# A hybrid encoder layer in float32: seven column blocks instead of four in the first stage of the feed-forward block, biases first, x by column blocks

## The chip, the cores and the metric

The kernel runs on one core of one Trainium2 chip. The metric is device time in microseconds (us) of one execution, as the median of several; lower is better. All arithmetic is float32: each large product is done on TensorE in three passes over operands that are split into a high and a low part.

## The reference

One encoder layer over 256 tokens of 2048 features (`SEQ` 256, `D_MODEL` 2048, `D_FF` 8192, one layer, so only the attention mixer occurs):

```python
mod = silu(c) @ mod_w + mod_b                       # 2048 -> 6 x 2048
sh_m, sc_m, g_m, sh_f, sc_f, g_f = split(mod, 6)
h = x * (1 + sc_m) + sh_m
x = layer_norm(ALPHA * x + (1 + g_m) * attention(h))  # q 32 heads, k and v 8 heads of 64, |q-k| <= 128, sink
h = x * (1 + sc_f) + sh_f
u = square(relu(h @ w1 + b1))                       # 2048 -> 8192
x = layer_norm(ALPHA * x + (1 + g_f) * (u @ w2 + b2)) # 8192 -> 2048
```

The weights are some 280 MB, read once: `mod_w` in 96 loads of 1 MB, the QKV matrix in 24, the output projection in 16, `w1` and `w2` in 64 each.

## The kernel before

**Weights.** Every weight comes as a 128x2048 float32 tile `raw` of 1 MB, issued in one fixed order on SP's queue (L580). Eight such buffers exist early, five later. For a matrix product each half of a tile is split: ScalarE copies it to the rounded high part `wh` (L638 while the order is written out, L627 later), VectorE subtracts to get the low part `wl` (L596). Five halves of each fit. A product of x and w is three matmuls, high by high, high by low, low by high (`mm3`, L925 to L927, 512 columns).

**Modulations.** A load of `mod_w` is used in one of two ways. As a *column*, VectorE multiplies it with the broadcast activation `cb` and sums along the row (`Col.step`, L742): one instruction for each load, which holds the scale, the shift or the gate of 128 features. As a *product*, TensorE does it (`Mod.quad`, L703, groups of 32 matmuls), with a small row turned afterwards. `MIXP` says which of the 16 attention feature tiles use the product, `FFP` how many per feature group of the feed-forward (before: two in group 2, so four product loads).

**Order written out by a planner.** `FLOW` is a hand-written list of loads: `"m"` two attention modulation loads, a number or `(g, p)` a QKV chunk, `"g"` and `"G"` the attention gate as column or product, `("o", c, j)` a chunk of the output projection, `"f"` and `"p"` a feed-forward modulation as column or product, `"x"` the rows of x for the residual, `"F"` a chunk of `w1`. `flow_order` takes that list with a table of costs (`COST`) and returns the order of every instruction on every engine up to the first `w1` chunks; the kernel issues them in exactly that order (`P` pins it). Where PE has nothing to do at the start and in the LayerNorm chain, dummy matmuls are issued (`idle`, L1041 and L1043).

**Biases.** The biases of QKV and of the output projection are added by a matmul with a selecting stationary operand (`bq`, L532), before as the last step of each sum.

**Attention, output projection, LayerNorm.** Scores (L1096), masking and maximum (L1105), exponential (L1113), scaling (L1136), transposes (L1142), values (L1161). The output projection is accumulated by 512-column block `c`; `gated_sum` forms gate times result (L1375), adds ALPHA x (L1377) and takes statistics (L1379). Then `norm_part`, `normed` (L1219, L1222), `ff_turn` transposes (L1280) and `ff_input` scales, splits (L1294, L1296, L1292) into the 16 input tiles of the feed-forward, by four feature groups.

**Feed-forward, first matrix.** The first 2048 hidden features (`w1a`) are done by *feature group*: chunk `W1A[n] = (kg, fq)` multiplies input group `kg` (512 features) with column block `fq` (512 hidden features) in the three-pass form with 256 columns (`w1a_unit`, L1316 to L1318), so that group 0 can start before groups 1 to 3 are there. Partial sums leave PSUM by L1329 (first) or L1326 (added), unless `KEEP` holds them there. The other hidden features are done tile by tile (`ff_hidden`): per input tile one 512-column matmul of `wh` with the high and low input side by side (L1539) and one 256-column matmul of `wl` (L1541), alternating eight and eight.

**Feed-forward, second matrix.** In four rounds (`BLK`) of 2048 hidden features, four chunks for each 512-column block `c` of the output (`ff_out`, again `mm3`). Between rounds the sums are added to `ys` (L1579, L1581). The last round is gated and normed while it ends.

Of the kernel before, what the change touches and what calls it, by code (L numbers as in the profile page):

```python
# [46 lines left out]
def mod_chunks():  # L47
# [8 lines left out]
    for which, p in (("m", GMP), ("f", 0)):  # L56
# [18 lines left out]
COST = dict(gP=1.01, gD=2.212, r=.2, c=.2, a=.1, H=.51, T=.33, S=.34, h=.96, l=1.137, u=1.36, e=.6, E=.48, sp=.85,  # L75
            cp=.48, bq=.5, rm=1.25, ra=1.2, ht=.43, hc=.48, sc=1.07, tt=.405, es=.2, ee=.1, ex=.49, rs=.19, rc=.09,
# [4 lines left out]
MODE = dict(u=0, w=0, bq=0, gP=2, sc=2, va=2)  # L81
TURN = (0.0, .11, .2, -.07, 0.0, .1, .15, .15, 0.0)
LATER = dict(gD=.3, gP=.1, u=.1, w=.1)
BANKS = dict(sum=6, gv=1, q=1, lt=2, wo=4, pm=1, sc=2, pt=2, po=1, w1=6)
W1A = [(0, 0), (0, 1), (0, 2), (0, 3), (1, 0), (1, 1), (1, 2), (1, 3),
       (2, 0), (2, 1), (2, 2), (2, 3), (3, 0), (3, 1), (3, 2), (3, 3)]
KEEP = ((0, 0), (0, 1), (2, 0), (2, 1))


def flow_loads():  # L90
# [3 lines left out]
    cols = [("gc", k) for k in range(4 * GMP, NK)]  # L94
    ff = [[v for v in ff_chunks() if v[2] == p] for p in range(2)]
    for v in FLOW:
# [5 lines left out]
        elif v == "g":  # L102
            out.append(cols.pop(0))
        elif v in ("f", "p"):
            out.append(("f",) + ff[v == "p"].pop(0))
        elif v == "x":
            out.append(("x",))
# [14 lines left out]
def flow_order():  # L122
# [28 lines left out]
    done, halves, freed, last, opened, out_of, summed = {}, [], [], {}, {}, {}, {}  # L151
    zs = [n for n in weights if type(n) is tuple and n[0] == "o"][-2:]
    for n in weights:
# [3 lines left out]
        for x in range(2):  # L157
            h, l = ("h", n, x), ("l", n, x)
            op(h, "ACT", "h", [("w", n)] + [("h",) + v for v in halves[-1:]], 1)
            op(l, "DVE", "l", [h] + [("l",) + v for v in halves[-1:]], 1, (), (), x == 1)  # L160
# [10 lines left out]
        for n, i in units:  # L171
            after = [("l", n, i % 2 if kind in "qz" else i // 2)] + last.get(kind == "u", [])
# [5 lines left out]
            elif kind == "w":  # L178
                kg, fq = W1A[n[1]]
                after += [("fc", kg, kp, x) for kp in range(2) for x in range(2)]  # L180
# [3 lines left out]
            if kind == "u" and k == 0:  # L184
                banks = ("sum",) * 2
            elif kind == "q" and i % 2 == 0:
                banks = ("q",)
            elif kind == "l" and i == 0 and n[1] not in opened:
                banks, opened[n[1]] = ("lt",) * 2, 1
            elif kind2 == "o" and i == 0 and n[1] not in out_of:  # L190
                banks, out_of[n[1]] = ("wo",) * 2, 0
            elif kind == "w" and (kg - 1, fq) not in KEEP and i % 2 == 0:
                banks = ("w1",)
            op(("u", n, i), "PE", "w" if kind == "w" else "u", after, 3, banks)
            if kind == "w" and (kg, fq) not in KEEP and i % 2:
                if fq in summed:
                    op(("ev", kg, fq, i // 2), "DVE", "ed", [("u", n, i), ("ev", summed[fq], fq, i // 2)], 1, (), ("w1",))
                else:
                    op(("ev", kg, fq, i // 2), "ACT", "ev", [("u", n, i)], 1, (), ("w1",))
# [9 lines left out]
            if kind == "u" and k == NK - 1 or kind == "l" and n[0] == 3 and i == 3:  # L209
                p = p if kind == "u" else n[1]  # L210
                op(("bq", p), "PE", "bq", [("u", n, i), ("sv",)], 1)
# [1553 lines left out]
```

## Time and profile before

| | |
|---|---|
| median of 3 runs | 1065.18 us (1064.52 to 1066.4) |
| profiled execution | 1064.04 us, span 1062.3 us |
| PE busy | 1041.4 us (98%) |
| DVE busy | 817.2 us (77%) |
| ACT busy | 535.9 us (50%) |
| POOL busy | 17.4 us (2%) |
| read from HBM | 288.5 MB |

PE is TensorE's matmul queue, DVE VectorE, ACT ScalarE, POOL GpSimd, SP the queue that issues the weight loads. A line such as `L742` is the kernel's line. Times in the views are microseconds from the start of the span, then the duration. "x8" means that so many instructions are merged in the row, and brackets at the end say how long the engine had been idle and what it waited for. Matmuls are pipelined and their ends modelled, so the distance of their starts, not their duration, is their price; a PE that is busy by the table may still have small gaps.

### The profile page before, as it was taken

The numbers are of one execution on the slowest core, as the hardware profiler recorded it, in microseconds if no ns is written. First come the engines' busy times: TensorE is split into PE (matmuls) and PEld (weight loads), VectorE is DVE, ScalarE is ACT, GpSimd is POOL, SyncE is SP. The second block draws the span as 40 slices with busy tenths as digits, with TensorE's granted clock in tenths as the row PEclk, the third lists the DMA queues.
The fourth block names the chain that finished last, engine by engine and source line by source line (L and its number), as shares of the span: only waits on it lengthen the run. The fifth ranks groups of instructions, "written<-read, shape, count | busy, mean of one in ns | idle before, by whom it ended". The sixth has DMA issues, their size and how long they took to land.

```text
span 1062.3 us, 15134 instructions
## 1 busy us (share of the span) xinstructions
PE 1041.4 (98%) x5955; PEld 872.2 (82%) x5955; DVE 817.2 (77%) x1137; ACT 535.9 (50%) x831; POOL 17.4 (2%) x41
## 2 busy tenths in 40 slices
PE   8899999999998999999999999999999999999997
PEld 6678787767886999888888888888888888888885
DVE  3989999999999999755778788666655566665795
ACT  4354469998335646633455543345443334454340
POOL 1000000000000000000000010000000000000000
PEclk9999999999999999999999999999999999999999
DMA  9999995589999997556877888856555555557512
GB/s 376 418 423 419 422 420 208 219 314 382 420 382 366 401 381 253 185 198 203 309 276 260 296 301 295 310 193 215 194 192 188 185 193 199 193 198 249 191 76 79
DMA packets 43463, 291.63 MB, mean 275 GB/s; under 512 B 4940, under 2 KB 5100, under 8 KB 9600
## 3 DMA queue, kind: packets, MB, share of 16 engines
q1 hardware_dynamic: 40256, 281.82, 70.2%
q0 software_dynamic: 2272, 7.40, 2.2%
q10 hardware_dynamic: 864, 1.45, 0.4%
q8 instruction: 46, 0.75, 0.3%
q14 instruction: 25, 0.20, 0.1%
HBM read 288.54 MB, written 2.11 MB: 274 GB/s over the span
## 4 chain that ended last, share of the span: by engine, by line
PE 70%; DVE 14%; DMA 11%; ACT 4%; issue 1%; DVEq 0%; ACTq 0%
PE pa L1539 17%; PE pa L925 12%; PE pa L927 12%; PE pa L926 12%; PE pa L1541 9%; DMA raw<-in_wqkv 6%; DVE raw L742 5%; DVE wl L596 4%; PE pa L1316 2%; PE pa L1318 2%; PE pa L1317 2%; DMA raw<-in_mod 2%; DMA raw<-in_wo 1%; DVE g L1105 1%; ACT g L1113 1%
## 5 line engine op out<-in xcount | busy, mean ns | idle before, releaser
L596 DVE TENSOR_TENSOR wl<-raw,wh 128x1024 fp32r<-128x1024 f32 x332 | 401.9, 1222 | 185.2 <-ACT wh L627 175.8
L627 ACT CAST wh<-raw 128x1024 fp32r<-128x1024 f32 x226 | 238.0, 1053 | 318.7 <-PE pa L927 184.5
L925 PE MATMUL pa<-wh,g 128*128 128x512 f32 x816 | 322.3, 395 | 2.0 <-ACT g L1021 1.4
L926 PE MATMUL pa<-wl,g 128*128 128x512 f32 x816 | 318.9, 391 | 2.0 <-DVE wl L596 2.0
L927 PE MATMUL pa<-wh,g 128*128 128x512 f32 x816 | 318.7, 391 | 1.0 <-DVE g L960 0.9
L1539 PE MATMUL pa<-g,wh 128*128 128x512 f32 x768 | 192.3, 392 | 0.0
L742 DVE CUSTOM_DVE_ANT_0 raw<-raw,cb 128x2048 f32<-128x2048 f32 x78 | 177.6, 2284 | 13.0 <-DMA raw<-in_mod 12.8
L925 PEld LDWEIGHTS pa<-wh,g 128*128 128x128 f32 x816 | 153.5, 188 | 39.2 <-issue 3.6
L927 PEld LDWEIGHTS pa<-wh,g 128*128 128x128 f32 x816 | 153.6, 188 | 34.3 <-DVE g L960 1.3
L926 PEld LDWEIGHTS pa<-wl,g 128*128 128x128 f32 x816 | 153.7, 188 | 33.6 <-DVE wl L596 2.8
L638 ACT CAST wh<-raw 128x1024 fp32r<-128x1024 f32 x106 | 109.5, 1052 | 100.0 <-PE pa L927 36.3
L1539 PEld LDWEIGHTS pa<-g,wh 128*128 128x128 f32 x768 | 138.3, 189 | 25.0 <-ACT wh L627 0.2
L1541 PEld LDWEIGHTS pa<-g,wl 128*128 128x128 f32 x768 | 104.8, 190 | 7.5
L1541 PE MATMUL pa<-g,wl 128*128 128x256 f32 x768 | 107.1, 282 | 0.0
L1316 PE MATMUL pa<-g,wh 128*128 128x256 f32 x256 | 72.8, 285 | 0.5 <-ACT g L1294 0.5
L1318 PE MATMUL pa<-g,wl 128*128 128x256 f32 x256 | 72.4, 283 | 0.0
L1317 PE MATMUL pa<-g,wh 128*128 128x256 f32 x256 | 72.4, 283 | 0.0
L1316 PEld LDWEIGHTS pa<-g,wh 128*128 128x128 f32 x256 | 49.1, 192 | 0.8 <-ACT g L1294 0.8
L1317 PEld LDWEIGHTS pa<-g,wh 128*128 128x128 f32 x256 | 49.1, 192 | 0.0
L1318 PEld LDWEIGHTS pa<-g,wl 128*128 128x128 f32 x256 | 49.1, 192 | 0.0
L1113 ACT ACTIVATE g<-g,nm 128x256 f32<-128x256 f32 x64 | 32.5, 530 | 1.2 <-DVE nm L1105 1.1
L1136 ACT ACTIVATE g<-g,rs 128x256 f32<-128x256 f32 x64 | 28.4, 532 | 0.0
(198 smaller groups left out, 695.0 us busy)
## 6 DMA issues: line engine op xcount, KB each, us to landing
raw<-in_mod SPq DMA_DIRECT2D x96, 1024.0 KB, 8.8
raw<-in_w SPq DMA_DIRECT2D x64, 1024.0 KB, 4.9
raw<-in_w1b SPq DMA_DIRECT2D x48, 1024.0 KB, 4.8
raw<-in_wqkv SPq DMA_DIRECT2D x24, 1024.0 KB, 16.3
raw<-in_wo SPq DMA_DIRECT2D x16, 1024.0 KB, 9.9
raw<-in_w1a SPq DMA_DIRECT2D x16, 1024.0 KB, 7.7
g<-in_x SPq DMA_DIRECT2D x4, 512.0 KB, 8.1
gb<-in_lnrow POOLq DMA_DIRECT2D x8, 256.0 KB, 5.5
```

Source lines behind the costliest of these rows:

```text
L596: self.pinned(nc.vector.tensor_sub(l, r, f32(self.hs[n])))
L627: self.last[n] = nc.scalar.copy(h, s)
L638: self.pinned(nc.scalar.copy(h, s))
L742: S.pinned(nc.vector.tensor_tensor_reduce(out=raw, in0=raw, in1=cb, scale=1.0, scalar=0.0, op0=OP.mult, op1=OP.add, accum_out=self.dst))
L925: S.pinned(nc.tensor.matmul(ps, xh, wh, start=start, stop=False))
L926: S.pinned(nc.tensor.matmul(ps, xh, wl, start=False, stop=False))
L927: S.prev = nc.tensor.matmul(ps, xl, wh, start=False, stop=stop)
L1316: S.pinned(nc.tensor.matmul(o, wh(w, 128), hh, start=new and fi + k == 0, stop=False))
L1317: S.pinned(nc.tensor.matmul(o, wh(w, 128), hl, start=False, stop=False))
L1318: S.pinned(nc.tensor.matmul(o, wl(w, 128), hh, start=False, stop=end and fi == 1 and k == 3))
L1539: nc.tensor.matmul(ps, wh(k, 128), ff_in(k), start=k == 0, stop=False)
L1541: nc.tensor.matmul(ps[:, :256], wl(k, 128), ff_in(k)[:, :256], start=False, stop=k == NK - 1)
```

## The change

1. `w1a` has seven column blocks (`NW1A` 7) in place of four: 28 chunks by feature group (7 for each group, in orders of their own, with new `KEEP`), and 36 hidden tiles in place of 48 in `ff_hidden`. The rounds of the second matrix take 3, 4, 5 and 4 chunks per column block (`BLOCKS`). The squares of blocks 0 to 2 follow their sums; those of blocks 3 to 6 come in the last column block of round 0. The columns of the second gate move from the second round to the third.
2. The first `w1a` chunk is done in halves of its input group, so that it begins when two of the group's four input tiles are there.
3. `FFP` is zero: all 32 feed-forward modulation loads are columns on VectorE. `MIXP` has tiles 0, 1, 2, 3, 10 in place of 0, 1, 2, 8, 12.
4. `FLOW` is new: the output projection's chunks come earlier in it, the feed-forward modulations later; 22 `w1` chunks are in it in place of 13.
5. The bias matmul opens a sum (`start`) in place of closing it; its loads and split come first.
6. x comes in four loads, one for each `"x"` in `FLOW`, from a layout with the column block outermost; before, one `"x"` issued four.
7. `ys` is loaded with the second bias directly, in eight broadcast loads on POOL's queue; before, two loads and an addition in the first round.
8. The table for the exponential is loaded by a one-element activation right after the sines.
9. `ff_hidden` does the 16 wide matmuls of a tile, then the 16 narrow ones.
10. Some costs of the planner change.

```diff
-BLK = 4
+NW1A = 7
+BLOCKS = ((0, 3), (3, 4), (7, 5), (12, 4))
-MIXP = tuple(int(k in (0, 1, 2, 8, 12)) for k in range(16))
+MIXP = tuple(int(k in (0, 1, 2, 3, 10)) for k in range(16))
-FFP = (0, 0, 2, 0)
+FFP = (0, 0, 0, 0)
 FLOW = [
+    "m", "m", 0, 1, "m", "m", (0, 4), 2, (0, 5), "m", "m", 3, "m", (0, 3), 4, "m", (1, 3), (1, 4), 5, "m", "m", 6,
+    (1, 5), "m", "m", (2, 4), (2, 3), "m", 7, 8, 9, "m", 10, (2, 5), "m", "m", 11, (3, 3), "g", "G", "g", (3, 4),
+    (3, 5), "G", "g", ("o", 2, 0), ("o", 1, 0), "g", "g", ("o", 2, 1), ("o", 1, 1), "g", ("o", 2, 2), "g", "g",
+    ("o", 1, 2), "G", "g", "g", ("o", 2, 3), "f", ("o", 1, 3), "G", "g", ("o", 3, 2), "g", "f", "f", ("o", 0, 2),
+    ("o", 3, 3), "x", "f", ("o", 3, 1), "f", ("o", 0, 3), "f", "x", ("o", 3, 0), ("o", 0, 1), ("o", 0, 0), "f", "F",
+    "f", "f", "F", "x", "f", "x", "F", "f", "F", "F", "F", "F", "F", "f", "f", "F", "f", "f", "f", "f", "f", "f",
...
-W1A = [(0, 0), (0, 1), (0, 2), (0, 3), (1, 0), (1, 1), (1, 2), (1, 3),
-       (2, 0), (2, 1), (2, 2), (2, 3), (3, 0), (3, 1), (3, 2), (3, 3)]
-KEEP = ((0, 0), (0, 1), (2, 0), (2, 1))
+W1A = [(k, c) for k, cs in enumerate(((0, 1, 2, 3, 6, 4, 5), (4, 5, 6, 0, 1, 2, 3),
+                                      (2, 3, 4, 5, 6, 0, 1), (0, 1, 2, 3, 4, 5, 6))) for c in cs]
+KEEP = ((0, 4), (0, 5), (1, 2), (1, 3), (2, 0), (2, 1))
...
-            P(nc.tensor.matmul(ps, pick[:, c:c + 1].to_broadcast([128, 128]), hl, start=False, stop=stop))
+            P(nc.tensor.matmul(ps, pick[:, c:c + 1].to_broadcast([128, 128]), hl, start=start, stop=False))
...
-            mm3(sums[p][t], hh[:, s], hl[:, s], wh(i), wl(i), k == 0, False)
+            mm3(sums[p][t], hh[:, s], hl[:, s], wh(i), wl(i), False, k == NK - 1)
...
-            nc.sync.dma_start(xs[c].rearrange("p (t n) -> p t n", t=NT), a["x"][:, :, c * 512:c * 512 + 512])
+        nc.sync.dma_start(xs[c], a["x"][c])
...
         kg, fq = W1A[n]
+        if n == 0:
+            kp, fp = i // 2, i % 2
+            if kp == 0:
+                opened[fq, fp] = bank()
+            for part in range(2):
+                for fi in range(2):
+                    o = opened[fq, fp][:, fi * 256:fi * 256 + 256]
+                    for k in (2 * kp, 2 * kp + 1):
+                        w = (2 * fp + fi) * 4 + k
...
             next(rotary)
+            if v[0] == 3:
+                P(nc.scalar.activation(warm, eps, AF.Exp))
...
+        if fq in early_u:
+            squared(fq, early_u[fq])
+        for c in ys_at.get(fq, ()):
+            ys[c] = (g4 if c == 3 else g4b)()
+            for t in range(NT):
+                nc.gpsimd.dma_start(part(ys, t, c), a["b2"][:, c * 512:c * 512 + 512].partition_broadcast(128))
...
-            for k8 in range(0, NK, 8):
-                for k in range(k8, k8 + 8):
-                    nc.tensor.matmul(ps, wh(k, 128), ff_in(k), start=k == 0, stop=False)
-                for k in range(k8, k8 + 8):
-                    nc.tensor.matmul(ps[:, :256], wl(k, 128), ff_in(k)[:, :256], start=False, stop=k == NK - 1)
-                S.done()
+            for k in range(NK):
+                nc.tensor.matmul(ps, wh(k, 128), ff_in(k), start=k == 0, stop=False)
+            for k in range(NK):
+                nc.tensor.matmul(ps[:, :256], wl(k, 128), ff_in(k)[:, :256], start=False, stop=k == NK - 1)
+                if k % 8 == 7:
+                    S.done()
...
-            for t, ps in enumerate(ff_out(blk, us, c)):
-                if blk == 0:
-                    nc.vector.tensor_add(part(ys, t, c), ps, bf(c))
-                else:
-                    nc.vector.tensor_add(part(ys, t, c), part(ys, t, c), ps)
+            for t, ps in enumerate(ff_out(us, n, c, later.get((blk, c), {}))):
+                nc.vector.tensor_add(part(ys, t, c), part(ys, t, c), ps)
```

More of the change, by code (lines that the diff above doesn't have):

```diff
@@ L94, in flow_loads @@
     cols = [("gc", k) for k in range(4 * GMP, NK)]
+    wo = [v[1] for v in FLOW if type(v) is tuple and v[0] == "o"]
+    xc = sorted(range(4), key=lambda c: 15 - wo[::-1].index(c))
     ff = [[v for v in ff_chunks() if v[2] == p] for p in range(2)]
@@ L149, in flow_order @@
         op(("S", k), "DVE", "S", [("H", k), ("T", k)], 0)
[L151 removed]
+    done, halves, freed, last, opened, begun, out_of, summed = {}, [], [], {}, {}, set(), {}, {}
     zs = [n for n in weights if type(n) is tuple and n[0] == "o"][-2:]
@@ L158, in flow_order @@
             h, l = ("h", n, x), ("l", n, x)
-            op(h, "ACT", "h", [("w", n)] + [("h",) + v for v in halves[-1:]], 1)
-            op(l, "DVE", "l", [h] + [("l",) + v for v in halves[-1:]], 1, (), (), x == 1)
+            w = "w" * (kind == "w" and n[1] < 4)
+            op(h, "ACT", "h" + w, [("w", n)] + [("h",) + v for v in halves[-1:]], 1)
+            op(l, "DVE", "l" + w, [h] + [("l",) + v for v in halves[-1:]], 1, (), (), x == 1)
             if len(halves) >= NHIGH:
@@ L179, in flow_order @@
                 kg, fq = W1A[n[1]]
-                after += [("fc", kg, kp, x) for kp in range(2) for x in range(2)]
+                after += [("fc", kg, kp, x) for kp in ((i // 2,) if f0 else range(2)) for x in range(2)]
             else:
@@ L447, in hybrid_kernel, with bias_rows, split, add @@
     posi, invf, snk = pack[:, 208:210].bitcast(I32), pack[:, 210:242], pack[:, 242:274]
+    def bias_rows(srcs):
+        raw, hl = g4()[:, :512], g4(F32R)[:, :512]
+        m = [n // 512 for _, n in srcs]
+        one, pick = cst.tile([128, sum(m)], F32, name="one"), cst.tile([128, sum(m)], F32R, name="pick")
+        nc.gpsimd.memset(raw, 0.0)
+        nc.gpsimd.memset(one, 0.0)
+        for p in (0, 32):
+            for (src, _), i, k in zip(srcs, (0, m[0]), m):
+                nc.gpsimd.dma_start(raw[p + i:p + i + k], src.rearrange("o (m n) -> (o m) n", m=k))
+            nc.gpsimd.affine_select(out=one, in_=one, compare_op=OP.not_equal, fill=1.0, base=-p,
+                                    pattern=[[-1, sum(m)]], channel_multiplier=1)
+        def split():
+            e = 32 + sum(m)
+            P(nc.vector.tensor_copy(pick, one))
+            P(nc.vector.tensor_copy(hl, raw))
+            P(nc.vector.tensor_sub(hl[32:e], raw[32:e], f32(hl[32:e])))
+        def add(ps, c, start):
+            P(nc.tensor.matmul(ps, pick[:, c:c + 1].to_broadcast([128, 128]), hl, start=start, stop=False))
+        return split, add
+    split_bias, bq = bias_rows(((a["bqkv"], QKV), (a["bo"], D)))
     ident = cst.tile([128, 128], F32, name="ident")
@@ L900, in hybrid_kernel @@
     assert all(m.planned == m.n for m in m_ff)
-    NF = FF // 128 // BLK
-    for blk in range(BLK):
-        for f in range(NF):
-            if blk:
-                if blk == 1 and f % 2:
+    last = len(BLOCKS) - 1
+    for blk, (c0, n) in enumerate(BLOCKS):
+        if c0 >= NW1A:
+            for f in range(4 * n):
+                if blk == 2 and f % 2:
                     if f == 1:
@@ L1360, in product, with bias @@
             late(*w, *n, i)
-    def bias(p):
+    def bias(p, t=None):
+        if t is not None:
+            quarter_of[0, p, t] = bank()
+            bq(quarter_of[0, p, t], CORD[p], True)
+            return
+        if p >= 3:
+            late_of[p] = banks()
         for t in range(NT):
-            bq((sums[p] if p < 3 else late_of[p])[t], CORD[p])
+            bq((sums[p] if p < 3 else late_of[p])[t], CORD[p], True)
+            late_begun.add((p, t))
     def row_bias(c):
@@ L1508, in square_halves, with squared @@
         nc.vector.tensor_sub(l, uf, f32(h))
+    def squared(c, tiles):
+        for fp in range(2):
+            u = tiles[fp](F32R)
+            square_split(uacc[c][:, fp * 512:fp * 512 + 512], c * 4 + fp * 2, 2, u, 0)
+            us_of.setdefault(c, []).append(u)
     g2 = None
-    us = []
-    for n in range(N1, 16):
+    us_of, ys = {}, {}
+    early_u = {0: (g4b, g4b), 1: (g4, g4), 2: (g4, g4b)}
+    ys_at = {3: (0, 1, 2), 4: (3,)}
+    for n in range(N1, 4 * NW1A):
         kg, fq = W1A[n]
@@ L1554, in ff_mm, with ff_out @@
             mm3(ps, u[:, :512][:, s], u[:, 512:][:, s], wh(k), wl(k), start and k == 0, stop and k == 3)
-    def ff_out(blk, us, c):
+    def ff_out(us, n, c, then={}):
         pss = [bank() for _ in range(NT)]
-        for kg in range(4):
+        for kg in range(n):
             w = S.main()
```

190 lines of the change are left out of this document (95 added, 95 removed), and 9 rows, old and new, of the table FLOW.

## Prediction

> **What bounds the kernel now.** I read the page's slices first, then the engines stretch by stretch (the windows view), then the chain of waits, then single engines in order of time round the place where the feed-forward starts.
>
> ```profile
> GB/s 376 418 423 419 422 420 208 219 314 382 420 382 366 401 381 253 185 198 203 309 276 260 296 301 295 310 193 215 194 192 188 185 193 199 193 198 249 191 76 79
> ...
> core 0: us, PE busy (x) PEld busy (x) DVE busy (x) ACT busy (x) POOL busy (x), PEclk, DMA share, GB/s
> 0.00:150.00 150.00, 141.71 (x880) 111.80 (x881) 120.72 (x157) 71.24 (x101) 4.99 (x20) 0.99 1.00 412
> 150.00:265.00 115.00, 113.69 (x813) 83.25 (x812) 109.97 (x261) 103.64 (x282) 0.00 (x0) 1.00 0.77 291
> 265.00:326.00 61.00, 60.90 (x268) 49.80 (x267) 58.74 (x66) 22.58 (x23) 1.61 (x3) 1.00 0.97 396
> 326.00:339.50 13.50, 8.53 (x128) 6.34 (x126) 11.99 (x29) 9.38 (x16) 0.00 (x0) 1.00 0.96 359
> 339.50:440.00 100.50, 99.96 (x813) 98.76 (x812) 97.17 (x124) 61.37 (x92) 1.05 (x2) 1.00 0.84 324
> 440.00:1062.00 622.00, 616.63 (x3065) 522.28 (x3063) 418.63 (x505) 267.65 (x321) 9.73 (x16) 1.00 0.62 217
> ...
> 1051.18 0.24 PE pa L927
> 1051.44 0.70 DVE g L1192
> ```
>
> Four stages. To 150 us the DMA queue is full (share 1.00): modulation and QKV weights. From 150 to 326 us (attention, output projection) PE is busy 174.6 of 176 us and DVE 168.7: both are nearly full. Then 13.4 us of LayerNorm chain. From 339.5 us PE runs the feed-forward without a gap to 1051.4 us, and 10.9 us of closing LayerNorm follow. So the time is the moment at which the feed-forward starts, plus its PE time, plus the close. What the change saves ahead of 339.5 us counts in full if PE stays fed afterwards.
>
> **Unit prices**, from starts to starts, since PE's durations overlap:
>
> ```profile
> 289.77 0.39 PE L925 MATMUL pa<-wh,g 128*128 128x512 f32 x1
> ...
> 309.49 0.63 PE L532 MATMUL pa<-g,pick 128*128 128x512 f32 x2
> ...
> 340.05 0.28 PE L1317 MATMUL pa<-g,wh 128*128 128x256 f32 x1
> 340.17 0.28 PE L1318 MATMUL pa<-g,wl 128*128 128x256 f32 x1
> ...
> 524.21 2.00 PE L1539 MATMUL pa<-g,wh 128*128 128x512 f32 x8
> 526.05 1.11 PE L1541 MATMUL pa<-g,wl 128*128 128x256 f32 x8
> 527.00 2.00 PE L1539 MATMUL pa<-g,wh 128*128 128x512 f32 x8
> ...
> 383.34 2.29 DVE L742 CUSTOM_DVE_ANT_0 raw<-raw,cb 128x2048 f32<-128x2048 f32 x1
> 385.55 1.22 DVE L596 TENSOR_TENSOR wl<-raw,wh 128x1024 fp32r<-128x1024 f32 x1
> 386.69 0.68 DVE L1326 TENSOR_TENSOR g<-g,pa 128x512 f32<-128x512 f32 x1
> 387.29 1.22 DVE L596 TENSOR_TENSOR wl<-raw,wh 128x1024 fp32r<-128x1024 f32 x1
> ```
>
> A 512-column matmul costs 0.227 us (87 of them in the 19.72 us from 289.77), a 256-column one 0.12, eight wide and eight narrow together 2.79. On DVE a modulation column (L742) costs 2.21, a low half (L596) 1.14, an addition to a partial sum (L1326) 0.60. A load of 1.05 MB takes 2.5 us at the 420 GB/s of the full slices.
>
> **Part by part.** Minus is a gain.
>
> *Order of loads before attention.* In the old list the last QKV load is the 60th of 1 MB, in the new one the 59th: -2.5 us where DMA limits. But chunk 11, on which the first scores hang, goes from place 52 to 53: +2.5. Product columns stay five. I take -1.0, being nearer the row of the full queue; ends -2.5 and +2.5.
>
> *Biases first.* Twelve of the twenty bias matmuls (L532) leave the ends of the QKV sums, some of them in the full stretch from 150 us, and open the sums at the start, where PE runs dummies:
>
> ```profile
> 11.80 2.97 PE L1041 MATMUL pa<-g 128*128 128x512 f32 x12
> ```
>
> 12 x 0.227 = 2.7 us. Six of them (the three early sums) fall beside those dummies; the other six fall between 20 and 60 us, beside loads. I take -2.0; ends 0 and -2.7. The bias loads move to the head of POOL's queue; the split of the biases (1.2 us of DVE) becomes a wait for the first product, with DVE busy little then.
>
> *Modulations of the feed-forward all on DVE.* Four PE products go. Each is one group of 32 (next fence: 1.0 us). One ran before 326 us: -1.0, ends -1.0 and 0. Its three fellows stood in the LayerNorm chain:
>
> ```profile
> 326.08 0.39 PE L927 MATMUL pa<-wh,g 128*128 128x512 f32 x1
> 328.10 1.08 PE L703 MATMUL pm<-raw,cact 128*32 128x128 f32 x32 [1.63 <-DMA raw<-in_mod]
> 332.38 1.08 PE L703 MATMUL pm<-raw,cact 128*32 128x128 f32 x32 [2.54 <-DMA raw<-in_mod]
> 333.39 2.34 PE L1043 MATMUL pa<-g 128*128 128x512 f32 x9
> 335.57 1.03 PE L1280 MATMUL pt<-ident,g 128*128 128x128 f32 x8
> 337.64 1.08 PE L703 MATMUL pm<-raw,cact 128*32 128x128 f32 x32 [0.80 <-DMA raw<-in_mod]
> 338.65 1.09 PE L1280 MATMUL pt<-ident,g 128*128 128x128 f32 x8
> ...
> 333.94 0.73 DVE L1222 TENSOR_SCALAR g<-g,mv,r 128x256 f32<-128x256 f32 x2
> 337.71 0.42 DVE L1292 TENSOR_TENSOR g<-g,g 128x256 fp32r<-128x256 f32 x1
> 338.05 1.22 DVE L596 TENSOR_TENSOR wl<-raw,wh 128x1024 fp32r<-128x1024 f32 x1
> 339.18 1.09 DVE L1292 TENSOR_TENSOR g<-g,g 128x256 fp32r<-128x256 f32 x3
> ```
>
> *LayerNorm chain.* The first transposes (335.57) stood behind nine dummies, and these behind a product that waited for its load; the normed rows were there at 334.7. The second transposes (338.65) stood behind the next product. Both waits go. Besides, the first feed-forward chunk is now taken in halves and needs only the first two input tiles, whose last operation could end near 338. I put the start 2.3 us earlier in the chain (0.9 from the first transposes, 1.4 from the halves); ends 0 and -4. What is late next is DVE, which puts a low half (338.05) among these operations.
>
> *Fewer modulations ahead of the feed-forward.* The old list has 13 feed-forward modulation loads before the last projection weight, the new one 6. DVE ran 47 columns by 326 us:
>
> ```profile
> 0.00:150.00 150.00, 50.08 (x44) 0.99 1.00 412
> 150.00:265.00 115.00, 34.16 (x30) 1.00 0.77 291
> 265.00:326.00 61.00, 22.90 (x20) 1.00 0.97 396
> ...
> 161.18 1.28 ACT L1113 ACT_TABLE_LOAD   x1
> 162.48 0.51 ACT L1113 ACTIVATE g<-g,nm 128x256 f32<-128x256 f32 x1
> ```
>
> (L742 by stretch; each column counts twice.) About six fewer x 2.21 = 13 us of DVE. But PE needs its own time: it was idle 1.4 us by the windows between 150 and 326, though ends of matmuls are modelled; the engine that is next, DVE, was idle 7.3 us. Hence -1.5, nearer PE's row than DVE's; ends +1.5 and -7. The exponential's table, now loaded early, is in this: 1.28 us of ACT at the first scores. The Trainium skill, page "ScalarE: Activation LUTs", section "What ACT_TABLE_LOAD costs", has about 2.66 us for a switch, drain included; here the load ended 0.02 us before the first exponential and no drain is seen. By the page the term would be 1.4 us larger at most, -2.9, and the sum -7.4.
>
> *Seven blocks in the three-pass form.* Twelve chunks of 48 narrow matmuls (5.76 us) replace twelve tiles of 2 x 2.79 = 5.58: +2.1. The wide and narrow runs of the remaining 36 tiles are now 16 long: eight wide take 1.84, eight at 0.227 would take 1.82, so one switch fewer saves 0.02: -0.8. Buffers are freed later in a tile, but five halves cover more than two tiles' lead: 0. Together +1.3, ends 0 and +2.5.
>
> *The longer first block.* Per feature group PE has 7 x 5.76 = 40.3 us of work where it had 23. DVE's part of a middle group: 14 low halves 16.0, 8 columns 17.7, about 2 for the inputs, 6 to 10 additions 3.6 to 6.0: 39 to 42. That is full, but the old stage (339.5 to 440) had DVE busy 97.17 of 100.5 us and PE 99.96, and DVE enters with some of the 13 us in hand. +0.5; ends 0 and +11 (second rival).
>
> *At nothing:* x in four loads (same bytes, needed only at the sums); the second bias by eight POOL loads into the sums (POOL idle, 20 us before use; if late, the first addition waits with six banks free); the rounds of 3, 4, 5, 4 (same 64 chunks, same additions); the late squares (DVE busy 67% after 440 us); the gate's 16 columns in the third round (20 tiles to hide 35 us of DVE).
>
> Sum: -1.0 - 2.0 - 1.0 - 2.3 - 1.5 + 1.3 + 0.5 = -6.0. The profiled execution took 1064.04 us; 1058.0 by its account. The median shown is 1065.18, 1.14 above it, so **1059.2**.
>
> **Rivals.** *DVE is the true limit up to 326 us.* The chain of waits between 150 and 326 us, by line, speaks for it:
>
> ```profile
> by line: DVE raw L742 19.9%; DVE wl L596 16.7%; DMA raw<-in_mod 11.3%; DMA raw<-in_wqkv 9.3%; DMA raw<-in_wo 9.0%; DVE g L1105 7.6%; ACT g L1113 6.6%; ACT g L1136 4.6%; issue 3.2%; DVE tmp L1375 2.1%; ACT wh L638 2.1%; DVE st L1379 2.0%; DV
> ```
>
> L742 and L596 lead it. PE's 174.6 of 176 us speak against. Then the relief is worth its end, -7, and the LayerNorm chain -4: sum -13, 1052.
>
> *Nothing gained ahead.* Three engines are tight from 150 to 265 (ACT 103.6, DVE 110.0, PE 113.7 of 115), all queues are in order, and a load late by the order written out takes back what the bias and the products gave. Then the LayerNorm term alone stands against the narrow form: -2.3 + 1.3 + 0.5, about 1064.7, no change.
>
> *Slower: a feature group comes late.* Place: the hand-over from group 1, 2 or 3 of the first matrix. If DVE enters the stage with no column in hand but with the chain's 12.0 us of work (its busy time from 326 to 339.5) still ahead, PE waits some 11 us over the three hand-overs: -6.5 + 11 = +4.5, 1069.7. It decides from 8.6 us of waits. Against it: PE and DVE were both at 97% and more in the old stage.
>
> *The clock.* PE loses its products in the 13 us gap and keeps dummies alone. The trace has one dip, in the first stage:
>
> ```profile
> 40.00:60.00 20.00, 18.57 (x73) 14.53 (x74) 19.68 (x21) 8.17 (x14) 0.00 (x0) 0.91 1.02 422
> ```
>
> 0.09 x 20 = 1.8 us; such a dip at the start of the feed-forward gives 1061.0. The Trainium skill, page "TensorE: Matmul & The Clock Gate", section "Part 1: The HAM clock gate", has PE at half clock after an idle window of 3.4 us: by that rule a gap without dummies pays this.
>
> **How the numbers follow.** Forecast (1055.5 to 1062) 0.44, with the clock's dip 0.06; DVE as the limit 0.16; nothing gained 0.18; a late group 0.16. 0.2% is 2.1 us, about what a measurement can tell. Faster 0.66, same 0.18, slower 0.16. The range leaves out the far half of the fast case and most of the late groups: 1051 to 1068.5; the forecast's own is 1055.5 to 1062.
>
> **What would show it.** The first three-pass matmul near 332 us instead of 339.5; no product between the last projection and the transposes, and that gap near 11 us; L532 at the start; the three-pass matmuls 0.12 us apart for 161 us with waits under 2 us at the hand-overs; then no gap to the last PE instruction near 1045. Wrong would be a start after 337 us, PE waiting on L1292 or L1294 in the first block, or wide matmuls no longer 0.227 apart.

## The result

The changed kernel took 1055.78 us (median of 4 runs, 1055.12 to 1056.02) beside 1064.85 us for the kernel before (4 runs): ratio 0.9913, 95% interval 0.9896 to 0.993. A second series on one chip with experiments gave 1055.86 us, ratio 0.9904 (0.9888 to 0.992). So it is 9 us faster (10 in the second series), where the prediction had 6. The profiled execution took 1055.99 us with a span of 1054.2 us, 8.1 us less span than before.

The windows view of the changed kernel, cut at its own stages (columns as in the prediction):

```profile
150.00:265.00 115.00, 113.59 (x789) 83.06 (x788) 113.55 (x266) 106.65 (x288) 0.52 (x1) 1.00 0.72 281
265.00:321.20 56.20, 55.15 (x244) 45.24 (x243) 53.75 (x63) 20.48 (x21) 1.09 (x2) 1.00 1.00 414
...
329.00:502.00 173.00, 172.32 (x1405) 170.67 (x1405) 152.03 (x176) 92.13 (x126) 4.25 (x8) 1.00 0.81 304
```

PE is about as full as before (113.59 of 115 us from 150 us, where it had 113.69; 55.15 of 56.20 from 265 us, where it had 60.90 of 61.00), and DVE is not less busy ahead of the LayerNorm chain: 113.55 of 115 us between 150 and 265, where it had 109.97. PE in order of time, from the last projection matmul (L939) to the first feed-forward matmuls, and the last of its form:

```profile
320.95 0.39 PE L939 MATMUL pa<-wh,g 128*128 128x512 f32 x1
321.18 4.70 PE L1056 MATMUL pa<-g 128*128 128x512 f32 x20
325.72 0.38 PE L1293 MATMUL pt<-ident,g 128*128 128x128 f32 x2
327.36 0.88 PE L1293 MATMUL pt<-ident,g 128*128 128x128 f32 x6 [1.25 <-DVE g L1235]
...
329.04 0.39 PE L1333 MATMUL pa<-g,wh 128*128 128x256 f32 x1
...
330.21 0.38 PE L1333 MATMUL pa<-g,wh 128*128 128x256 f32 x1 [0.68 <-ACT g L1307]
...
1042.91 0.40 PE L939 MATMUL pa<-g4b,g 128*128 128x512 f32 x1
```

No product stands in the gap. The last projection matmul is 5.1 us earlier than before (326.08), the first three-pass matmul 10.5 us earlier (339.50). DVE in the same stretch, and below it DVE's corresponding step in the trace of before, the product of the last projection's second half:

```profile
315.53 2.27 DVE L753 CUSTOM_DVE_ANT_0 raw<-raw,cb 128x2048 f32<-128x2048 f32 x1
...
320.27 1.22 DVE L607 TENSOR_TENSOR wl<-raw,wh 128x1024 fp32r<-128x1024 f32 x1
...
322.31 0.68 DVE L1411 TENSOR_TENSOR tmp<-pa,g 128x512 f32<-128x512 f32 x1
...
324.86 1.21 DVE L607 TENSOR_TENSOR wl<-raw,wh 128x1024 fp32r<-128x1024 f32 x1
...
326.89 0.73 DVE L1235 TENSOR_SCALAR g<-g,mv,r 128x256 f32<-128x256 f32 x2
```

```profile
329.36 0.68 DVE L1375 TENSOR_TENSOR tmp<-pa,g 128x512 f32<-128x512 f32 x1
```

Before, DVE came to that product 3.1 us after PE's last projection matmul had passed (326.31); now it comes 1.1 us after it (321.18). The span falls apart like this (starts of rows, us; the last three-pass matmul is counted to where the next row starts, 1051.24 before and 1043.14 after):

| stretch | before | after | change | forecast |
|---|---|---|---|---|
| to the last projection matmul | 326.08 | 320.95 | -5.1 | -5.5 |
| gap to the first three-pass matmul, and the wait just behind it | 13.4 + 0 | 8.1 + 0.84 | -4.5 | -2.3 |
| from there to the end of the last matmul of that form, without that wait | 711.7 | 713.3 | +1.5 | +1.8 |
| close | 11.1 | 11.1 | 0 | 0 |
| sum | 1062.3 | 1054.2 | -8.1 | -6.0 |

### The profile page after: what moved, and what is told of

It is laid out like the page before. It is cut to its first block, busy times and chain, and to the rows that moved or that the text cites. A ratio compares the mean times of both kernels' runs of the same rounds, so it can differ in the third digit from the quotient of the medians.

```text
span 1054.2 us, 15275 instructions
## 1 busy us (share of the span) xinstructions
PE 1037.9 (98%) x6028; PEld 880.3 (84%) x6028; DVE 827.0 (78%) x1135; ACT 537.7 (51%) x831; POOL 20.6 (2%) x47
## 4 chain that ended last, share of the span: by engine, by line
PE 73%; DVE 16%; ACT 5%; DMA 3%; issue 2%; SPq 0%; DVEq 0%; POOL 0%; ACTq 0%
PE pa L938 13%; PE pa L937 13%; PE pa L939 13%; PE pa L1589 12%; PE pa L1591 7%; DVE raw L753 5%; DVE wl L607 5%; PE pa L1346 5%; PE pa L1345 5%; PE pa L1347 5%; ACT g L1126 2%; DMA raw<-in_wqkv 1%; ACT g L1149 1%; DMA g<-rowm 1%; DVE g L1072 1%
## 5 line engine op out<-in xcount | busy, mean ns | idle before, releaser
L607 DVE TENSOR_TENSOR wl<-raw,wh 128x1024 fp32r<-128x1024 f32 x332 | 399.3, 1221 | 142.6 <-ACT wh L638 113.1
L937 PE MATMUL pa<-wh,g 128*128 128x512 f32 x672 | 265.8, 396 | 1.5 <-ACT wh L649 0.9
L938 PE MATMUL pa<-wl,g 128*128 128x512 f32 x672 | 263.0, 391 | 2.4 <-DVE wl L607 2.4
L939 PE MATMUL pa<-wh,g 128*128 128x512 f32 x672 | 262.5, 391 | 0.0
L753 DVE CUSTOM_DVE_ANT_0 raw<-raw,cb 128x2048 f32<-128x2048 f32 x82 | 186.8, 2284 | 8.4 <-DMA raw<-in_mod 8.0
L937 PEld LDWEIGHTS pa<-wh,g 128*128 128x128 f32 x672 | 126.4, 188 | 32.1 <-issue 4.3
L938 PEld LDWEIGHTS pa<-wl,g 128*128 128x128 f32 x672 | 126.5, 188 | 29.7 <-DVE wl L607 4.7
L939 PEld LDWEIGHTS pa<-wh,g 128*128 128x128 f32 x672 | 126.4, 188 | 26.6
L1589 PE MATMUL pa<-g,wh 128*128 128x512 f32 x576 | 137.5, 391 | 0.0
L1589 PEld LDWEIGHTS pa<-g,wh 128*128 128x128 f32 x576 | 106.0, 188 | 20.8 <-issue 0.2
L1345 PE MATMUL pa<-g,wh 128*128 128x256 f32 x432 | 122.5, 284 | 0.0
L1347 PE MATMUL pa<-g,wl 128*128 128x256 f32 x432 | 122.3, 283 | 0.0
L1346 PE MATMUL pa<-g,wh 128*128 128x256 f32 x432 | 122.2, 283 | 0.0
L1346 PEld LDWEIGHTS pa<-g,wh 128*128 128x128 f32 x432 | 82.9, 192 | 0.0
L1345 PEld LDWEIGHTS pa<-g,wh 128*128 128x128 f32 x432 | 82.9, 192 | 0.0
L1591 PE MATMUL pa<-g,wl 128*128 128x256 f32 x576 | 74.7, 283 | 0.0
L937 PE MATMUL pa<-wh,g4b 128*128 128x512 f32 x144 | 56.1, 389 | 0.0
L938 PE MATMUL pa<-wl,g4b 128*128 128x512 f32 x144 | 56.1, 389 | 0.0
```

Of the source, the lines that this page charges most:

```text
L607: self.pinned(nc.vector.tensor_sub(l, r, f32(self.hs[n])))
L753: S.pinned(nc.vector.tensor_tensor_reduce(out=raw, in0=raw, in1=cb, scale=1.0, scalar=0.0, op0=OP.mult, op1=OP.add, accum_out=self.dst))
L937: S.pinned(nc.tensor.matmul(ps, xh, wh, start=start, stop=False))
L938: S.pinned(nc.tensor.matmul(ps, xh, wl, start=False, stop=False))
L939: S.prev = nc.tensor.matmul(ps, xl, wh, start=False, stop=stop)
L1345: S.pinned(nc.tensor.matmul(o, wh(w, 128), hh, start=new and fi + k == 0, stop=False))
```

## The experiments

All times below are medians of 4 to 6 runs, in three series on different chips. The kernel before took 1065.85 to 1066.34 us in them; the changed kernel was in one of them, with 1055.86 us, and the differences below are taken from that.

**The changed kernel again.**

> The changed kernel itself, beside the others on one chip, so that their times can be set against it. Expected: 0.9913 of the kernel before as measured first, within its interval of 0.9896 to 0.993. What varies from run to run should show as the stretch with granted clock 0.83 in the first 60 us, which its first profile has and other profiles of it lack: without it the last projection matmul is at about 320.1 us instead of 320.95.

1055.86 us; last projection matmul at 320.84, first three-pass matmul at 328.94, granted clock 0.83 from 20 to 30 us. The expectation that other profiles lack this dip fell: this one has it again. Of six other kernels with the same loads up to there (whole chunk, no dummies, the two reordered chains, products, no early table) one has such a dip; their last projection matmul lies between 319.5 and 320.3 us. A difference of up to 1.5 us at that place between two single profiles is therefore not read as an effect below. Behind the first three-pass matmul profiles agree far better: to the end of the last one it is 714.1 us in both profiles of the changed kernel.

**The first chunk taken whole.**

```
-        if n == 0:
+        if False:                       # w1a_unit: no halves
...
+    move(("u", ("w1", 0), 0), ("u", ("w1", 0), 1), after=("fc", 0, 1, 1))
```

(`move` takes keys out of the list `KEYS` and puts them in at the place named.)

> The changed kernel with its first feed-forward chunk taken whole again: its matmuls start only when all four input tiles of the feature group are there. Theory (the time of the start counts in full, since PE then runs to its last matmul without a gap): in the changed kernel's trace the last input operation ends at 332.99 us, the first three-pass matmul is at 329.04 and 0.84 us of waits follow, so PE does 3.1 us of work before 332.99; the chunk taken whole starts at 333.0 and the time grows by 2.5 to 3.3 us, to about 1058.7. Rival (the start does not set the end, because PE waits later for DVE at the hand-over from group 0 to group 1, and the early work only moves that wait): within 0.5 us of 1055.8, and a new gap or a vanished one in PE's sequence near 369 us.

1056.98 us, 1.1 us slower (ratio 0.992, 0.9906 to 0.9933). The start itself did not move, since the whole chunk also begins with the first input tile; PE then waits twice for DVE's inputs:

```profile
329.71 0.38 PE L1354 MATMUL pa<-g,wh 128*128 128x256 f32 x1 [0.98 <-DVE g L1313]
...
332.37 0.38 PE L1354 MATMUL pa<-g,wh 128*128 128x256 f32 x1 [0.85 <-DVE g L1313]
```

From the first three-pass matmul to the first matmul of the second matrix it takes 1.8 us longer (166.8 us where the changed kernel has 165.0), and none of it is made up later. So the halves are worth 1.1 us by the medians and 1.8 by the trace, and they save waits behind the start, not the start; the theory was right in kind, and too high in size because it took the start as barred until the last input.

**Biases last.** The twelve QKV bias matmuls go back to the ends of the sums, with the flags that begin and end a sum.

```
-            mm3(sums[p][t], ..., wh(i), wl(i), False, k == NK - 1)
+            mm3(sums[p][t], ..., wh(i), wl(i), k == 0, False)
...
+    KEYS = [k for k in KEYS if k[0] != "bq"]
+    for p in range(6):
+        KEYS.insert(min(i for i, k in enumerate(KEYS) if k[:2] == ("E", p)), ("bq", p))
```

> The changed kernel with the QKV biases added at the end of each sum again (twelve matmuls of 512 columns, 0.227 us each, moved from the first 60 us back to the ends of the sums); the order of loads stays the new one. Theory of the prediction: those twelve lie on PE's full stretch when they come last and beside dummies and waits when they come first: slower by 2.0 us, ends 1.0 and 2.7. Rival (the gain of 4.4 us in PE's lost time that the two traces show up to 60 us is the order of the loads alone, and PE has loose places after 60 us as well, where 9.2 us are lost up to the last projection matmul): within 0.7 us of the changed kernel.

1058.23 us, 2.4 us slower (ratio 0.9932, 0.9919 to 0.9946). PE in order of time:

```profile
322.67 0.39 PE L943 MATMUL pa<-wh,g 128*128 128x512 f32 x1
```

The last projection matmul comes 1.8 us later than at 320.84, and the stretches behind it are equal (gap 8.05 us). The prediction's term of 2.0 holds; the two ratios' intervals only just meet (0.9919 here, 0.992 for the changed kernel), but all runs here (1057.65 us and more) lie above all runs of the changed kernel (1056.32 and less). What the order of loads, the product gone and the rest gave is the distance that is left: 326.08 to 322.67, 3.4 us.

**No dummies in the gap.**

```
-        if free and FILL.get(key):
+        if free and FILL.get(key) and spare is None:
```

> The changed kernel without the twenty and the four dummy matmuls that fill PE's gap between the output projection and the feed-forward. PE then does nothing from 321.2 to 327.4 us but two transposes of 0.4 us. Rival of the prediction (the clock dips after such a gap): a window of 10 us with granted clock 0.83, as the stretch from 20 to 30 us shows it, at the start of the feed-forward, and 1.7 us more, 1057.5. Trainium skill, page 'TensorE: Matmul & The Clock Gate', section 'Part 1: The HAM clock gate': half clock after an idle window of about 3.4 us until about 3.4 us of activity, an estimate of 1.7 us as well. Other theory (the gap is too short or the clock is not what sets the start): granted clock 1.00 and within 0.4 us of 1055.8.

1056.94 us, 1.1 us slower. PE in order of time, and the first ten microseconds of the feed-forward in the windows view:

```profile
326.44 1.54 PE L1293 MATMUL pt<-ident,g 128*128 128x128 f32 x6 [3.62 <-DVE g L1235]
...
329.89 0.41 PE L1333 MATMUL pa<-g,wh 128*128 128x256 f32 x1
330.11 0.41 PE L1334 MATMUL pa<-g,wl 128*128 128x256 f32 x1
...
332.01 0.28 PE L1333 MATMUL pa<-g,wh 128*128 128x256 f32 x1
332.12 0.28 PE L1334 MATMUL pa<-g,wl 128*128 128x256 f32 x1
```

```profile
328.00:338.00 10.00, 9.50 (x65) 9.20 (x66) 8.39 (x12) 6.13 (x11) 0.00 (x0) 0.80 0.64 246
```

After 3.62 us without work the first matmuls are 0.21 us apart instead of 0.12 until 332.0, and the granted clock of the stretch is 0.80, where the changed kernel has 1.00. The slow matmuls from 328.1 to 331.8 us, some sixteen at 0.09 us more each, cost 1.4 us, and the wait for the second input is 0.3 us shorter (0.39 us, where the changed kernel has 0.68): together 1.1. The Trainium skill, page "TensorE: Matmul & The Clock Gate", section "Part 1: The HAM clock gate", has half clock after an idle window of about 3.4 us and for about as long a time of work. The trace agrees in the idle time and the half rate; the slow stretch is longer, 5.5 us from 326.44, of which the feed-forward has the last 3.7; and in the run of eights below a wait of 1.95 us was enough. The twenty-four dummies of the changed kernel are what kept that rival away.

**The chain reordered.**

```
...
+    move(("ff", 1, 2, 0), before=("ff", 1, 3, 0))
+    move(("l", ("w1", 0), 0), after=("v2", 0))
+    move(("l", ("w1", 0), 1), before=("tm", 0, 1))
+    move(("nx", 2, 1), before=("nx", 3, 1))
+    FILL["ft", 0, 0], FILL["u", ("w1", 0), 0] = 17, 2
```

> The changed kernel with the DVE work round the LayerNorm chain put in another order: the modulation column at 315.53 us (2.2 us) behind the feed-forward's first chunk, the two low halves that stand inside the chain at 320.27 and 324.86 ahead of it, one normalisation of ScalarE (0.75 us) behind the inputs of group 0, and 17 and 2 dummies where 20 and 4 were. Theory (DVE's order sets the start of the feed-forward): the normed rows come 1.5 us earlier, the first three-pass matmul near 327.3 instead of 329.04, the wait of 0.68 us behind it is shorter, and the time falls by 1.5 to 2.2 us to about 1053.9. Rival (what DVE puts off comes due at the first hand-over, where PE needs group 1 after 40 us): PE waits there for up to 2.2 us and the time stays within 0.5 us of 1055.8.

1053.42 us (1053.03 to 1054.01), 2.4 us faster than the changed kernel; ratio to before 0.9887 (0.9873 to 0.99). PE, then DVE, in order of time:

```profile
319.55 0.39 PE L951 MATMUL pa<-wh,g 128*128 128x512 f32 x1
...
324.76 0.87 PE L1305 MATMUL pt<-ident,g 128*128 128x128 f32 x6 [0.74 <-DVE g L1247]
...
325.98 0.39 PE L1345 MATMUL pa<-g,wh 128*128 128x256 f32 x1
...
327.27 0.38 PE L1345 MATMUL pa<-g,wh 128*128 128x256 f32 x1 [0.80 <-ACT g L1319]
```

```profile
320.49 0.69 DVE L1423 TENSOR_TENSOR tmp<-pa,g 128x512 f32<-128x512 f32 x1
...
324.30 0.73 DVE L1247 TENSOR_SCALAR g<-g,mv,r 128x256 f32<-128x256 f32 x2
```

From the product to the normed rows 3.81 us instead of 4.58 (322.31 to 326.89), and the product itself comes 0.4 us sooner after PE: 1.2 us come from DVE's order, as the theory has it. The gap is 6.4 us instead of 8.1; the other 0.5 us lie between the transposes and the first matmul, where two dummies fewer stand. The wait behind the start did not shrink (0.96 us by starts). No wait appears at a hand-over. Another 0.7 us of the time lie ahead of the projection's end, where single profiles differ by more. This version beats both kernels.

**One step more.**

```
+    move(("l", ("w1", 1), 0), ("l", ("w1", 1), 1), after=("fc", 0, 1, 1))
```

> The reordered LayerNorm chain (three DVE steps and one ScalarE step moved, fewer dummies) with one more step: the two low halves of the second feed-forward chunk go behind the inputs of group 0 instead of standing ahead of and among them. Theory (in the first reordered version PE waits 0.96 us behind its first matmuls because ScalarE's second input waits for a DVE input that stands behind a low half of 1.1 us): that wait falls to 0.2 us or less and the time to about 2.9 us under the changed kernel. Rival (the second input waits for ScalarE itself, or the second chunk then waits for its low halves): no more than 0.3 us under the first reordered version, 2.2 us under the changed kernel.

1055.26 us: 1.8 us slower than the first reordered version (whose runs all lie below its runs). The wait behind the start stayed (0.84 us by starts), so the low half was not its cause; and PE waits in the second chunk, as the rival had it:

```profile
341.48 0.38 PE L1360 MATMUL pa<-g,wl 128*128 128x256 f32 x1 [1.82 <-DVE wl L607]
```

DVE's low half for that matmul stands behind a modulation column that waited 3.5 us for its load.

**The old order of loads in the changed kernel.** `FLOW` and `MIXP` of before, with x four times in its one place and "p" replaced by "f".

> The changed kernel with the old order of loads and the old five product columns (0, 1, 2, 8, 12); the x rows are asked for in one place, as before, and the four products of the feed-forward's modulations stay gone. So 13 of those modulations stand ahead of the last projection weight again instead of 6. Theory from the two traces (the first 60 us lose 21.3 us of PE with the old order and 16.9 with the new one, 1.7 of it the biases; and DVE enters the LayerNorm chain 2 us late with the old order): last projection matmul about 2.5 us later, gap behind it 1.5 to 2 us longer, together +4 to +4.5, about 1060. The prediction's own terms (load order -1.0, fewer modulations -1.5): +2.5, 1058.3. Rival (DVE is the limit up to the projection's end): 7 columns of 2.21 us come back, +7 or more, with waits of PE for L607 between 150 and 320 us.

1085.39 us, 19.5 us slower than the kernel before and 29.5 slower than the changed one: far outside both sums. The rival's "+7 or more" covers the number, but its sign is absent: between 150 us and the projection's end PE waits nowhere for L607. The last projection matmul is at 334.78 and the gap 23.9 us:

```profile
343.43 14.57 PE L1056 MATMUL pa<-g 128*128 128x512 f32 x63
357.84 1.04 PE L1293 MATMUL pt<-ident,g 128*128 128x128 f32 x8
358.63 0.36 PE L1333 MATMUL pa<-g,wh 128*128 128x256 f32 x1
```

With this list the orders of PE and DVE come out otherwise too: the transposes of groups 1 and 2 stand ahead of the first chunk, and those of group 2 behind 63 dummies, because the planner puts them after that group's modulations; DVE works through seven columns between 342 and 359 us. So the run prices one ill-fitting combination and does not isolate the term "order of loads". What part of the 13.9 us ahead of the projection's end is order and what is DVE stays open.

**Products to columns, alone, in the kernel before.**

```
-FFP = (0, 0, 2, 0)
+FFP = (0, 0, 0, 0)     # and "p" in FLOW becomes "f"
```

> The kernel before with one edit: the four products of the feed-forward's modulations are columns on DVE instead. Theory of the prediction (PE's products, waiting for their loads, hold up dummies and transposes in the LayerNorm chain): one product of 1.0 us less ahead of the last projection matmul, and the gap behind it shrinks from 13.4 to about 11 to 12 us, together 2 to 3.3 us faster. Rival (the gap is set by DVE, which begins the chain late with its columns and low halves, and four more columns on DVE make that no better): gap within 0.7 us of 13.4, and no more than 1.0 us gained.

1076.47 us, 10.6 us slower (ratio 1.0097, 1.0081 to 1.0113). Both theories looked at the wrong place. PE in order of time, then the last stretch in the windows view, then DVE at the last projection's product and at the normed rows:

```profile
327.55 5.15 PE L1044 MATMUL pa<-g 128*128 128x512 f32 x22
...
333.64 1.85 PE L1281 MATMUL pt<-ident,g 128*128 128x128 f32 x14 [0.72 <-DVE g L1223]
...
336.94 0.28 PE L1317 MATMUL pa<-g,wh 128*128 128x256 f32 x1
...
406.98 0.55 PE L1317 MATMUL pa<-g,wh 128*128 128x256 f32 x1 [3.83 <-DVE g L1327]
...
421.66 1.44 PE L1317 MATMUL pa<-g,wh 128*128 128x256 f32 x5 [6.28 <-ACT g L1295]
...
423.84 0.41 PE L1318 MATMUL pa<-g,wh 128*128 128x256 f32 x1
424.05 0.41 PE L1319 MATMUL pa<-g,wl 128*128 128x256 f32 x1
```

```profile
380.00:425.00 45.00, 34.89 (x256) 34.28 (x255) 41.30 (x55) 18.55 (x27) 1.05 (x2) 0.86 0.90 340
```

```profile
328.60 0.68 DVE L1376 TENSOR_TENSOR tmp<-pa,g 128x512 f32<-128x512 f32 x1
...
333.18 0.73 DVE L1223 TENSOR_SCALAR g<-g,mv,r 128x256 f32<-128x256 f32 x2
```

The gap shrank as the first theory said, by 3.8 us to 9.6. But the four columns more made DVE late in the hand-over to the last feature groups: PE waits 3.8 us at 403 us for an addition that stands behind a column, and 6.3 us at 415 us for the inputs of a group whose modulations are not done, and after each wait it runs at 0.21 us a matmul. From the first three-pass matmul to the last of PE the stretch is 15.1 us longer.

**The same swap undone in the changed kernel.** `FFP = (0, 0, 2, 0)`, and the 17th, 19th, 21st and 23rd "f" of `FLOW` become "p".

> The changed kernel with the four products of the feed-forward's third modulation group on PE again, at the same places in the load list (now beside the feed-forward, not in the LayerNorm chain). DVE has four columns of 2.21 us less to do. Theory (with seven blocks PE is the bound from the feed-forward's first matmul on and DVE keeps up): four groups of 1.0 us and two transposes lie on PE's full stretch, +4.0 to +4.4, about 1060. Rival (DVE is still as short as in the kernel before, where the same four columns on DVE cost 10.6 us): no change, or up to 2 us faster.

1061.01 us, 5.2 us slower (ratio 0.9952, 0.994 to 0.9964). From the first three-pass matmul to the first matmul of the second matrix PE takes 171.2 us instead of 165.0: four products of 1.0 us from start to start, 1.5 us of waits for two of their loads, and 0.7 us that were not taken apart:

```profile
364.25 1.08 PE L715 MATMUL pm<-raw,cact 128*32 128x128 f32 x32 [0.41 <-DMA raw<-in_mod]
...
377.81 1.08 PE L715 MATMUL pm<-raw,cact 128*32 128x128 f32 x32 [0.78 <-DMA raw<-in_mod]
```

In this kernel, with seven blocks, PE is the bound from its first feed-forward matmul on; in the kernel before, with four, it was DVE as soon as the products were gone. The two kernels differ in the order of loads as well, and no run takes the blocks alone away, so that the blocks make the difference is argued and not shown.

**DVE relieved by force.**

```
+            n = 64 if self in short else 2048
+            raw, c = raw[:, :n], cb[:, :n]
...
```

(`short`: the eight columns of group 0 and three of group 1; the kernel leaves out most of their sums.)

> The changed kernel with eleven modulation columns of the feed-forward (all eight of group 0, three of group 1) taken over 64 of 2048 elements only: this leaves out most of those sums, while loads, order and buffers stay. DVE loses some 23 us of work ahead of 320 us. Rival of the prediction (DVE is the true limit up to the projection's end): the last projection matmul comes 7 us earlier or more, so the time is 7 to 13 us shorter. Theory (PE is the bound from 150 us, and DVE's relief is worth what PE still loses to it): the one wait of 1.1 us at 313 us goes, and in the LayerNorm chain the column at 315.5 us that stands ahead of it: projection's end 1 to 2 us earlier, gap 0.5 to 1 us shorter, together -1.5 to -3.

1052.97 us, 2.9 us faster than the changed kernel (ratio to before 0.9874, 0.9859 to 0.989). The stage before the projection's end in the windows view, then PE and DVE in order of time:

```profile
265.00:320.00 55.00, 55.00 (x244) 45.47 (x243) 36.85 (x66) 21.02 (x22) 1.10 (x2) 1.00 1.01 415
```

```profile
319.43 0.39 PE L942 MATMUL pa<-wh,g 128*128 128x512 f32 x1
...
326.59 0.39 PE L1336 MATMUL pa<-g,wh 128*128 128x256 f32 x1
```

```profile
319.86 0.69 DVE L1414 TENSOR_TENSOR tmp<-pa,g 128x512 f32<-128x512 f32 x1 [0.54 <-PE pa L942]
```

DVE falls to 36.85 of 55 us, and PE, now at 55.00 of 55, ends the projection 1.4 us earlier; about 1.0 of this is PE's one wait for a low half of DVE, near 314 us in the changed kernel, which is gone. The gap is 0.9 us shorter, because DVE now waits for PE and its last product comes 0.2 us after PE has passed instead of 1.1. Some 23 us of DVE are worth 2.9 us: PE is the bound there but for that wait, and the first rival is refuted.

**Runs of eight.** The hidden blocks' matmuls alternate eight wide, eight narrow, as before.

> The changed kernel with the wide and narrow matmuls of the later hidden blocks in runs of eight again instead of sixteen (36 tiles). Prediction's term: one switch of width less per tile saves 0.02 us, 36 tiles, so going back costs 0.8 us. Rival (the switch costs nothing, or the earlier freeing of buffers in the eights gives it back): within 0.3 us of the changed kernel.

1056.48 us, 0.6 us slower, with intervals that overlap (0.9896 to 0.9921 against 0.9888 to 0.992). The trace is clearer: from the first three-pass matmul to the end of the last one PE takes 714.8 us, 0.7 us more than in the changed kernel, for 36 tiles. In order of time, runs of sixteen in the changed kernel:

```profile
646.38 3.79 PE L1589 MATMUL pa<-g,wh 128*128 128x512 f32 x16
...
651.91 3.82 PE L1589 MATMUL pa<-g,wh 128*128 128x512 f32 x16
...
657.48 3.82 PE L1589 MATMUL pa<-g,wh 128*128 128x512 f32 x16
```

The first two tiles take 5.53 and 5.57 us; in runs of eight they take 5.56 and 5.58 (starts at 647.15, 652.71 and 658.29). That is 0.02 us a tile, as the term had it: 0.7 us for 36 tiles, 0.8 were forecast.

The profiled run of this kernel is its slowest (1057.46 us), and its projection ends at 322.66, though its code is that of the changed kernel up to there:

```profile
314.54 0.50 PE L938 MATMUL pa<-wl,g 128*128 128x512 f32 x1 [1.95 <-DVE wl L607]
```

The wait for DVE's low half, 1.05 us in the changed kernel, is 1.95 us here, and from 315.8 to 319.2 us the matmuls of 512 columns are 0.43 us apart instead of 0.227 (granted clock 0.79 from 315 to 323). So this place varies from one execution to the next, and a longer wait there costs its own length and then a slow stretch.

**No early table.**

```
-            if v[0] == 3:
-                P(nc.scalar.activation(warm, eps, AF.Exp))
```

> The changed kernel without the exponential run early on one column, so that ScalarE loads the exponential's table at the first scores again, as before. Theory (in the trace of before the load took 1.28 us and ended 0.02 us before the first exponential, on a ScalarE busy 106.65 of 115 us in that stretch, with PE's waits for L1149 only 0.3 us at a time): between 0 and 1.3 us slower, most likely 0.5. Trainium skill, page 'ScalarE: Activation LUTs', section 'What ACT_TABLE_LOAD costs': 2.66 us with its drain; by that estimate up to 2.7 us slower.

1054.99 us, not slower (ratio 0.9894, 0.9881 to 0.9908; the changed kernel's interval overlaps). ScalarE in order of time:

```profile
160.41 1.28 ACT L1126 ACT_TABLE_LOAD   x1
162.51 0.51 ACT L1126 ACTIVATE g<-g,nm 128x256 f32<-128x256 f32 x1 [0.82 <-DVE nm L1118]
```

The load is back at the first scores and nobody waits for it: the first exponential waits for DVE. The 2.66 us that the Trainium skill gives on its page "ScalarE: Activation LUTs", section "What ACT_TABLE_LOAD costs", appear nowhere in the time.

## Why the prediction was right in sign and 3.4 us short

**Ahead of the projection's end: -5.5 forecast, -5.1 measured.** Biases first measured 1.8 us at that place and 2.4 in the time, for a term of 2.0. The remaining 3.4 us stand against 3.5 for order, product and relief together. No run separates the three, but the traces say where they lie. Counting what PE loses from start to start beyond its unit prices, with dummies as lost time, the kernel before loses 24.7 us up to 60 us and the run with biases last 22.1; from 60 us to the projection's end both lose 34.8. So about 2.6 us come from the start, where the order of loads is new (forecast 1.0), the product's own time is 1.0, and DVE's relief (forecast 1.5) leaves no trace ahead of the projection's end. That the sum came out is in part luck. The term "fewer modulations" rested on loads counted in the lists. What counts is columns done, here in the windows view of L753 (each counts twice):

```profile
0.00:150.00 150.00, 50.03 (x44) 0.99 1.00 412
150.00:265.00 115.00, 31.87 (x28) 1.00 0.72 281
265.00:321.20 56.20, 20.64 (x18) 1.00 1.00 414
```

45 columns by the projection's end, where the kernel before ran 47: two fewer and not six, 4 us of DVE and not 13.

**The LayerNorm chain: the step that failed**, -2.3 forecast, -4.5 measured, past the stated end of -4. The prediction had one part for the transposes (0.9) and one for the halves (1.4), and placed DVE's relief ahead of the chain. By its steps, from the rows above and those of the prediction (us):

| step | before | products gone alone | after | reordered |
|---|---|---|---|---|
| PE's last projection matmul passed, to DVE's last product | 3.1 | 1.0 | 1.1 | 0.7 |
| to the normed rows | 4.6 | 4.6 | 4.6 | 3.8 |
| to the transposes that need them | 1.6 | 0.5 | 0.5 | 0.5 |
| to the first three-pass matmul | 3.9 | 3.3 | 1.7 | 1.2 |
| wait just behind it | 0 | 0.5 | 0.8 | 1.0 |

The transposes' part measured 1.2. The fourth row less the new wait is 1.4 us, the figure that the prediction had for the halves, but that is luck: the chunk taken whole starts just as early. What moved the start there is that the product (1.0 us) and the transposes of group 1 no longer stand between; the halves save 1.1 to 1.8 us of waits behind the start. Missing was the first row, 1.9 us: DVE came to the last product 3.1 us behind PE, because it had begun the chain of the first half late, and in the changed kernel it comes only 1.1 us behind. The run with short columns shows that DVE's work sets this row: there it is 0.2 us. In the run with the products gone the lateness is gone too, in part because PE itself ends the projection 1.2 us later there. It could be read from the trace of before (the product at 329.36, PE at 326.31); the prediction looked for the delay in PE's queue and named DVE only as what is late next.

**The feed-forward: +1.8 forecast, +1.5 measured.** The narrow form costs what it was said to, and the hand-overs cost nothing. But the prediction priced the seven blocks at +1.3 and the missing products at -1.0 as if they were separate. They are not: in the kernel before, with four blocks, the same move to DVE costs 10.6 us, by the mechanism and nearly at the price of the prediction's rival of a late group (3.8 and 6.3 us of waits, forecast 11); in the changed kernel undoing it costs 5.2. The likely reason is that the seven blocks give DVE time for its four extra columns, and that this is where the longer first block pays; the order of loads, which differs too, was not ruled out.

**The base.** 1.14 us were added because the median shown lay above the profiled run. After the change the two agree (1055.78 and 1055.99), so of the 3.4 us by which the forecast was high 2.1 belong to the sum and the rest to this.

The clock did not dip, thanks to the dummies; "nothing gained ahead" is refuted by the projection's end.

## What to carry to other kernels

When a gap between two stages is costed, follow every engine's queue into it: here the product and the dummies ahead of the first transposes held up 1.2 us, and DVE's arriving late another 1.9 that the forecast did not have. Work that is moved from the full engine to one nearly full has no price of its own: the same four columns cost 10.6 us in one kernel and saved 5.2 in another. Cost such an edit together with the edits that give the other engine time. And before a wait is blamed on the operation that stands ahead of it, take that operation away: the wait behind the feed-forward's start outlived the low half that seemed to cause it.

## What the runs showed of the hardware

- A PE that waited 3.6 to 6.3 us with nothing to run came back at about half its rate (0.21 us a 256-column matmul instead of 0.12) for 4.3 to 5.5 us. After a wait of 1.95 us a stretch of 3.4 us at half rate began 1.3 us later (in the run of eights); after one of 1.82 us none came (second reordered chain). The gap filled with dummies shows none.
- Some 10 us with granted clock 0.83 lie in the first 60 us of nine of the fourteen profiles of these kernels and are absent from five. Among kernels with the same loads, the run of eights left aside, the projection ends at 320.2 to 321.0 us with it and at 319.5 to 320.3 without; that it is the cause is not shown.
- The load of the exponential's table, 1.28 us, cost nothing on a ScalarE that was busy 106.65 of 115 us in that stage with the table loaded early.
